# Operand sums of the second FFN weight, made between the steps of the projections instead of inside the FFN loop

## The chip, the cores and the metric

One core of one Trainium2 chip runs the kernel. The metric is the device time in microseconds (us); of several runs, the median. Engines: TensorE (PE; its weight loads PEld), VectorE (DVE), ScalarE (ACT), GpSimd (POOL), and SyncE (SP), which here only issues transfers.

## What is computed

One layer of an encoder with 1024 tokens and 16 meta tokens ahead of them, width 1024, in float32: neighbourhood attention (8 heads) beside gated linear attention (GLA, 4 heads), then an FFN with a convolution of width 3 over the tokens and a gate.

```python
u = rmsnorm(h, norm_mix_pre)
proj = u @ w_in
o_na = rmsnorm(neighbourhood_attention(q_na, k_na, v_na, rpb), na_gain)
o_gl = gla_bidirectional(q_gl, k_gl, v_gl, g_gl, z_gl, ...)   # per direction, chunks of 64:
#   ds = einsum(k_end, v); S[n+1] = decay[n] * S[n] + ds[n]; o = a @ v + q_dec @ S
h = h + rmsnorm(concat(o_na, o_gl) @ w_o, norm_mix_post)
a = conv3(rmsnorm(h, norm_ffn_pre) @ w_ffn_in)                # 2 * 2816 columns
y = (gelu(a[:, 2816:]) * a[:, :2816]) @ w_ffn_out
return (h + rmsnorm(y, norm_ffn_post))[16:]
```

## The kernel before, in words

Large products are float32 split in a high and a low part, three products each. A program of named steps writes the work; a scheduler with a time model then sets each engine's order, and each engine runs its own list in order.

**Projections and heads** (0 to some 374 us). `load_w` (L157) brings blocks of w_in by SP in two halves, `split` makes high and low parts (ScalarE L148, VectorE L149). The tuple `T0` (L67) gives the order of the steps: "gqk" projects queries and keys of a pair of GLA heads (products pk, pq; ScalarE copies them to gst at L347, VectorE multiplies at L350), "exp" makes decays (GpSimd L322 to L327 write bl and ga), "head" is `gla_head` (L357): GpSimd zeroes two columns of the state tile S (L365, L366), TensorE transposes keys (gtm, gt) and makes the 16 chunk products (gd), VectorE runs the scan over the chunks in both directions (L396 on partitions 0 to 63, L400 on 64 to 127, 15 operations each on 64x128), and TensorE takes the states for gom (L409) and go (L429, L432). go begins with a matmul of zeros (zbf, L425). "qk" and "v" are projections of the neighbourhood heads; `v_windows` (L489) copies values to vw_d in HBM by SP.

**FFN loop** (`for j`, L1113; some 690 to 1098 us). The first FFN weight is multiplied by a seven-product scheme over 22 column blocks j. `prep` makes operand sums bt (GpSimd L941 to L944) and splits them (ScalarE L922, VectorE L924). TensorE makes the products (L966 to L968) into q_r, q_x, q_z; ScalarE evicts (c, L1079), VectorE adds (L1130, L1140, L1146), convolves (L1014, L1015) and multiplies by the gelu (ScalarE L1025) at L1026; y goes to y_d.

**Operand sums of the second weight.** The second product, too, is made by seven products per pair of blocks, from y_d, s_d (sums of y) and t_d (sums of w_ffn_out). After each odd j, `t_sums(j // 2)` (L1085) loads two blocks of 512 KB of w_ffn_out by SP (L1088), makes four differences in place on GpSimd (L1090 to L1093, 128x512 each) and stores both to t_d by SP (L1095); `s_sums` (L1097) does the like with y. The tiles come from a ring of six, tag "y", which also holds y. There are eleven calls. t_d is read only in the sweeps after the loop, from 1098 us on.

Of the kernel before, what the change touches and what calls it, by code (L numbers as in the profile page):

```python
# [8 lines left out]
F32 = mybir.dt.float32  # L9
F32R = mybir.dt.float32r  # L10
BF16 = mybir.dt.bfloat16
# [4 lines left out]
P = 128  # L16
# [7 lines left out]
NFC = FF // P  # L24
# [26 lines left out]
def _mask_offsets():  # L51
# [13 lines left out]

PRIO = {(0, 0): 5, (0, 2): 20, (0, 3): 2, (1, 0): 1, (1, 2): 60, (1, 3): 2, (2, 1): 20, (2, 3): 5, (3, 2): 1, (3, 3): 60}
T0 = (  # L67
    "gqk 0", "head 0", "qk 2", "exp 2", "head 1", "exp 3", "qk 0", "v 0", "gqk 1", "head 2", "qk 1", "head 3",
    "n15",
)  # L70
T1 = ("qk 3", "na 0 0", "na 0 1", "v 1", "na 1 0", "na 1 1")
T2 = (
# [10 lines left out]
def kernel(ctx: ExitStack, tc: tile.TileContext, a: dict):  # L83
    nc = tc.nc
    mm = nc.tensor.matmul
# [7 lines left out]
    t_d = [dram.tile([2, 2, P, 512], F32, name=f"t_d{k}") for k in range(NFC // 2)]  # L93
# [60 lines left out]
    ul = up.tile([P, KC, L], F32R, name="ul")  # L154
    wp = t1.enter_context(tc.tile_pool(name="wp", bufs=3))

    def load_w(src, w, name):  # L157
        hs, ls = [], []
        for kh in range(2):
            raw = wp.tile([P, 4, 256], F32, tag="wr", name=f"{name}_r{kh}", bufs=2)  # L160
            nc.sync.dma_start(raw[:, :, :w], src[:, 4 * kh : 4 * kh + 4, :])
            hi = wp.tile([P, 4, 256], F32R, tag="wh", name=f"{name}_h{kh}")
            lo = wp.tile([P, 4, 256], F32R, tag="wl", name=f"{name}_l{kh}")
            split(hi[:, :, :w], lo[:, :, :w], raw[:, :, :w])
            hs.append(hi)
            ls.append(lo)
        return hs, ls
# [40 lines left out]
    with tc.tile_pool(name="p1", bufs=2) as p1:  # L208
        g_pre = p1.tile([P, D], F32, name="g_pre", bufs=1)
        nc.sync.dma_start(g_pre, a["norm_mix_pre"].broadcast_to([P, D]))  # L210
        for i in range(9):
            n = NM if i == 0 else P
# [46 lines left out]
    gwh = gp.tile([P, HGL, P], F32R, name="gwh")  # L259
    gwl = gp.tile([P, HGL, P], F32R, name="gwl")  # L260
    split(gwh, gwl, gwr)
    zbf = gp.tile([P, 512], BF16, name="zbf")
    nc.gpsimd.memset(zbf, 0.0)
    maskf = gp.tile([P, 512], I8, name="maskf")
    maskv = maskf.rearrange("p (t c) -> p t c", c=P)
# [5 lines left out]
    d0 = gp.tile([P, L], BF16, name="d0")  # L271
# [85 lines left out]
    def gla_head(hd):  # L357
# [53 lines left out]
        for g in range(2):  # L411
            at = asb[g]
            pf = ps_s(f"gaf{hd}_{g}")
            pb = ps_s(f"gab{hd}_{g}")
            for t in range(4):
                c = slice(NM + (4 * g + t) * P, NM + (4 * g + t + 1) * P)
                mm(pf[:, t * P : (t + 1) * P], B[:64, c], C[:64, c], start=True, stop=True)
                mm(pb[:, t * P : (t + 1) * P], B[64:, c], C[64:, c], start=True, stop=True)
            atv = at.rearrange("p (t c) -> p t c", c=P)
            pbv = pb.rearrange("p (t c) -> p t c", c=P)  # L420
            nc.scalar.copy(atv[:64, :, :64], pbv[:64, :, :64])
            nc.scalar.copy(atv[64:, :, 64:], pbv[64:, :, 64:])
            nc.vector.copy_predicated(at, maskf, pf)
            po = ps_c(f"go{hd}_{g}")
            mm(po, zbf[:, :P], zbf, start=True, stop=False, skip_group_check=True)  # L425
            for t in range(4):
                i = 4 * g + t
                tc_ = slice(t * P, (t + 1) * P)
                mm(po[:, tc_], V[:, i, :], at[:, tc_], start=False, stop=False, skip_group_check=True)  # L429
                for s in range(2):  # L430
                    cc = NM + i * P + 64 * s
                    mm(  # L432
                        po[:, t * P + 64 * s : t * P + 64 * s + 64],
                        S[:, 2 * i + s + 1, :],
                        C[:, cc : cc + 64],
                        start=False,
                        stop=(t == 3 and s == 1),
                        skip_group_check=True,
                    )
            gla_norm(po, mgl[:, hd, 1 + 512 * g : 513 + 512 * g], 512, f"gn{hd}_{g}")  # L440
# [48 lines left out]
    def v_windows(half):  # L489
        vv = v_d[:, 256 * half : 256 * half + 256].rearrange("(r c) d -> r c d", c=64)  # L490
        for b in range(4):
            nr, r0 = BNR[b], BR0[b]
            for q in range(4):
# [5 lines left out]
                else:  # L499
                    nc.sync.dma_start(dst[0], vv[0, cols, :])  # L500
                    nc.sync.dma_start(dst[1:], vv[r0 + 1 : r0 + 1 + nr, cols, :])

    hs, ls = load_w(a["w_in_b"][5], 256, "wvg1")
    pv = lambda i0, i1: [proj_v1(i, hs, ls, vg_d, 256, "pvg1") for i in range(i0, i1)]
    gla_gate(0)
# [13 lines left out]
    def step1(name):  # L519
        op, *n = name.split()  # L520
        n = [int(x) for x in n]
        if op == "na":
            na_step(*n)
        elif op == "n15":
            gla_norm(o15s, mgl[:, :, 0], HGL, "gn15")
        elif op == "v":
            na_v(n[0], na_meta if n[0] else None)
        else:
            steps[op](*n)

    for name in T0:
        step1(name)
    t1r.close()

    frp = ctx.enter_context(tc.tile_pool(name="frp", reuse_waits="tile", bufs=1, side="right"))

# [545 lines left out]
    def ring4(name):  # L1082
        return fc.tile([P, 4, 256], F32, tag="y", name=name, bufs=6)

    def t_sums(k):  # L1085
        w = [ring4(f"w{k}_{c}").rearrange("p (h d) b -> p h (d b)", h=2) for c in range(2)]
        for c in range(2):
            nc.sync.dma_start(w[c], a["w_ffn_out"][2 * k + c].rearrange("h p d -> p h d"))  # L1088
        b11, b12, b21, b22 = w[0][:, 0], w[0][:, 1], w[1][:, 0], w[1][:, 1]
        nc.gpsimd.tensor_sub(b11, b12, b11)  # L1090
        nc.gpsimd.tensor_sub(b12, b22, b12)
        nc.gpsimd.tensor_sub(b22, b22, b11)
        nc.gpsimd.tensor_sub(b21, b21, b22)  # L1093
        for c in range(2):
            nc.sync.dma_start(t_d[k][c].rearrange("h p d -> p h d"), w[c])  # L1095

    def s_sums(k, p, q):  # L1097
        (a11, a21), (a12, a22) = p, q
        nc.gpsimd.tensor_add(a22, a21, a22)
# [13 lines left out]
    for j in range(1, NFC):  # L1113
        if j == NFC - 1:
            t = mixp.tile([P, 8, HC], F32, tag="m", name="pre1")
            raws = [t[:, x, :512] for x in range(8)]
            for w in (4, 5):
                t = quad(w, f"pre{w}", F32)
                raws += [t[:, x, :512] for x in range(4)]
            for k in range(8):  # L1120
                pre.append(raws[2 * k : 2 * k + 2])
                nc.sync.dma_start(pre[k][0], y_d[2 * k][0])
                nc.sync.dma_start(pre[k][1], a["w_ffn_out"][2 * k][0])
        R, X = acc1[j, "r"], acc1[j, "x"]
        c11 = evac("c11", j, "r")
        y = ring4(f"y{j}")
        y = [y[:, :2], y[:, 2:]]
        ys.append(y)
        prod(j, 6, "r", False)
        nc.vector.tensor_add(c11, X[:, :, :258], c11)  # L1130
        c12 = evac("c12", j, "r")
        prod(j, 5, "z", True)
        Z = acc1[j, "z"]
        conv(j, 0, c11, y[0])
        prod(j, 7, "r", False)
        c22 = evac("c22", j, "r")
        if j < NFC - 1:
            prep(j + 1)
            prod(j + 1, 1, "r", True)
        nc.vector.tensor_add(c22, Z[:, :, :258], c22)  # L1140
        prod(j, 4, "r", False)
        if j < NFC - 1:
            prod(j + 1, 2, "x", True)
        prod(j, 3, "z", False)
        conv(j, 0, R[:, :, :258], y[1])
        nc.vector.tensor_add(c12, Z[:, :, :258], c12)  # L1146
        gated(j, 1, c22, y[1])
        gated(j, 0, c12, y[0])
        store(y_d[j], y)
        if j % 2:  # L1150
            t_sums(j // 2)
            s_sums(j // 2, ys[j - 1], y)
    fcs.close()
    fas.close()
# [260 lines left out]
```

## Time and profile before

| | us |
|---|---|
| median of 3 runs (lowest, highest) | 1353.88 (1353.38, 1354.87) |
| the profiled execution | 1352.37 |
| its span, first to last instruction | 1350.7 |

| engine | busy, us | share of the span |
|---|---|---|
| PE | 1268.2 | 94% |
| DVE | 914.0 | 68% |
| ACT | 619.3 | 46% |
| POOL | 429.7 | 32% |

The mean granted TensorE clock is 0.973 of full speed. Shares are averages over stages with different limits, so they are read stage by stage: a timeline gives each instruction's start and length and, in brackets, how long its engine sat idle before it and what released it. "SPq" and the like are an engine's sequencer issuing transfers.

### The profile page before, as it was taken

What the parts mean: (1) busy time and instruction counts of PE and PEld (TensorE: products, weight loads), DVE (VectorE), ACT (ScalarE), POOL (GpSimd) and SP (SyncE); (2) the same over time, 40 slices, a digit from 0 to 9 for tenths busy, and PEclk for the clock granted to TensorE, in tenths of its full rate; (3) what the DMA queues carried; (4) which work ended last, traced back from release to release, by engine and by line L of the source; (5) the groups of instructions that cost most, each with busy time, mean ns of one, the idle gap of its engine ahead of it and who ended that gap; (6) DMA issues with size and microseconds to landing.
All of it is one profiled execution on the core that took longest, in us unless ns stands there. A gap on an engine that the chain in (4) does not pass through costs nothing.

```text
span 1350.7 us, 23581 instructions
## 1 busy us (share of the span) xinstructions
PE 1268.2 (94%) x9048; PEld 1139.0 (84%) x9050; DVE 914.0 (68%) x1453; ACT 619.3 (46%) x1198; POOL 429.7 (32%) x401
## 2 busy tenths in 40 slices
PE   7979999999997899998779999999999999999997
PEld 6869888988886587776779999999999998888876
DVE  6491365254544577865979898898888978555556
ACT  5443544152332555656544444344443444545542
POOL 1260001000021154432556565765657633000001
PEclk9989999999988889999889999999999999999999
DMA  6311132351187545842134434444344456866735
GB/s 204 119 38 50 34 93 84 110 177 64 51 270 225 208 132 197 278 137 94 40 117 149 142 124 164 167 154 143 124 164 159 154 173 228 303 198 207 247 125 187
DMA packets 117137, 203.74 MB, mean 151 GB/s; under 512 B 18080, under 2 KB 51200, under 8 KB 117024
## 3 DMA queue, kind: packets, MB, share of 16 engines
q1 hardware_dynamic: 117024, 202.24, 44.6%
q8 instruction: 71, 1.16, 0.4%
q14 instruction: 42, 0.34, 0.1%
HBM read 145.64 MB, written 66.19 MB: 157 GB/s over the span
## 4 chain that ended last, share of the span: by engine, by line
PE 63%; DVE 18%; DMA 6%; ACT 5%; issue 5%; POOL 1%; SPq 1%; DVEq 0%; ACTq 0%; POOLq 0%
DVE bl L924 5%; PE bank L1202 4%; PE bank L1201 4%; PE bank L1200 4%; PE q_r L966 3%; PE q_r L967 3%; PE q_r L968 3%; PE ops L694 2%; PE pna L175 2%; PE pna L176 2%; PE pna L177 2%; DVE g L1015 2%; PE pp L688 2%; PE wo L766 2%; PE wo L767 2%
## 5 line engine op out<-in xcount | busy, mean ns | idle before, releaser
L966 PE MATMUL q_r<-ah,bh 128*128 128x258 f32 x504 | 145.4, 288 | 14.9 <-ACT c L1079 14.9
L967 PE MATMUL q_r<-al,bh 128*128 128x258 f32 x504 | 144.3, 286 | 0.0
L968 PE MATMUL q_r<-ah,bl 128*128 128x258 f32 x504 | 143.9, 285 | 0.0
L966 PEld LDWEIGHTS q_r<-ah,bh 128*128 128x128 f32 x504 | 97.1, 193 | 17.2 <-ACT c L1079 17.1
L149 DVE TENSOR_TENSOR ol<-r,oh 128x512 fp32r<-128x512 f32 x116 | 74.6, 688 | 46.0 <-ACT oh L148 46.0
L1200 PE MATMUL bank<-oh,oh 128*128 128x512 f32 x264 | 102.9, 390 | 2.2 <-DVE c L1266 2.2
L1201 PE MATMUL bank<-oh,ol 128*128 128x512 f32 x264 | 102.7, 389 | 0.0
L1202 PE MATMUL bank<-ol,oh 128*128 128x512 f32 x264 | 102.2, 389 | 0.0
L966 PE MATMUL q_z<-ah,bh 128*128 128x258 f32 x336 | 95.4, 284 | 6.3 <-DVE y L1015 4.9
L1025 ACT ACTIVATE g<-g 128x512 f32<-128x512 f32 (+1 forms) x46 | 28.2, 614 | 157.0 <-DVE g L1015 156.9
L967 PEld LDWEIGHTS q_r<-al,bh 128*128 128x128 f32 x504 | 97.0, 193 | 0.0
L968 PEld LDWEIGHTS q_r<-ah,bl 128*128 128x128 f32 x504 | 97.0, 192 | 0.0
L967 PE MATMUL q_z<-al,bh 128*128 128x258 f32 x336 | 95.2, 283 | 0.0
L968 PE MATMUL q_z<-ah,bl 128*128 128x258 f32 x336 | 95.0, 283 | 0.0
L148 ACT CAST oh<-r 128x512 fp32r<-128x512 f32 x116 | 65.6, 619 | 50.2 <-PE bank L1201 40.0
L924 DVE TENSOR_TENSOR bl<-bt,bh 128x512 fp32r<-128x512 f32 x84 | 85.2, 1015 | 3.5 <-ACT bh L922 3.5
L924 DVE TENSOR_TENSOR bl<-fr,bh 128x512 fp32r<-128x512 f32 x67 | 64.5, 966 | 17.4 <-ACT bh L922 17.2
L1011 ACT ACTIVATE g<-c,vec 128x512 f32<-128x512 f32 (+1 forms) x46 | 36.6, 795 | 75.2 <-DVE c L1140 40.8
L966 PEld LDWEIGHTS q_z<-ah,bh 128*128 128x128 f32 x336 | 63.9, 190 | 6.7 <-issue 5.1
L144 POOL TENSOR_TENSOR rsc_r<-rsc_v,nhalf 128x1 f32<-128x1 f32 x8 | 5.8, 725 | 197.5 <-DVE rsc_v L143 197.5
L1014 DVE SCALAR_TENSOR_TENSOR g<-c,vec,g 128x512 f32<-128x512 f32 (+1 forms) x46 | 53.5, 1164 | 17.1 <-ACT g L1011 17.1
L1026 DVE TENSOR_TENSOR y<-y,g 128x512 f32<-128x512 f32 (+1 forms) x46 | 54.9, 1194 | 13.4 <-ACT g L1025 13.3
(388 smaller groups left out, 4257.9 us busy)
## 6 DMA issues: line engine op xcount, KB each, us to landing
fr<-in_w_ffn_in_dram SPq DMA_DIRECT2D x44, 512.0 KB
y_d<-y SPq DMA_DIRECT2D x44, 256.0 KB
w<-in_w_ffn_out_dram SPq DMA_DIRECT2D x22, 512.0 KB
t_d<-w SPq DMA_DIRECT2D x22, 512.0 KB
s_d<-y SPq DMA_DIRECT2D x44, 256.0 KB
r<-s_d SPq DMA_DIRECT2D x44, 256.0 KB
r<-t_d SPq DMA_DIRECT2D x44, 256.0 KB
r<-y_d SPq DMA_DIRECT2D x25, 256.0 KB
```

The lines of the kernel that those rows point to most:

```text
L148: nc.scalar.copy(hi, src)
L149: nc.vector.tensor_tensor(lo, src, hi.bitcast(F32), ALU.subtract)
L924: nc.vector.tensor_tensor(lo, src, hi.bitcast(F32), ALU.subtract)
L966: mm(ps, w[0][:, k, :], A[0][:, k, c], start=(first and k == 0), stop=False, skip_group_check=True)
L967: mm(ps, w[0][:, k, :], A[1][:, k, c], start=False, stop=False, skip_group_check=True)
L968: mm(ps, w[1][:, k, :], A[0][:, k, c], start=False, stop=(last and k == 3), skip_group_check=True)
L1011: nc.scalar.activation(dst, tap(1), AF.Identity, bias=col(VEC_CB + ch), scale=col(VEC_CONV + 2 * NFC + ch))
L1014: nc.vector.scalar_tensor_tensor(dst, tap(0), col(VEC_CONV + ch), dst, ALU.mult, ALU.add)
L1026: nc.vector.tensor_mul(val, val, g)
L1200: mm(ps, A[0][:, tk], B[0], start=first, stop=False, skip_group_check=True)
L1201: mm(ps, A[1][:, tk], B[0], start=False, stop=False, skip_group_check=True)
L1202: mm(ps, A[0][:, tk], B[1], start=False, stop=last, skip_group_check=True)
```

## The change

`t_sums` moves out of the loop. In `T0` there are twelve new steps "t 0" to "t 11" between the old ones. Step "t k" first stores set k - 1 from ScalarE's queue (L517), then loads set k on SP behind the last weight load (L523) and makes the four differences on GpSimd (L525 to L528). `issue_after` ties a transfer to the place of the named instruction in the program, so that the scheduler does not move it ahead. The tiles are a pool of their own, four of 128x2x512, that is two sets of two; it is closed after the stage. To make room, zbf shrinks to 128 columns, and the zeroing matmul takes d0 as its other operand.

```diff
 T0 = (
-    "gqk 0", "head 0", "qk 2", "exp 2", "head 1", "exp 3", "qk 0", "v 0", "gqk 1", "head 2", "qk 1", "head 3",
-    "n15",
+    "gqk 0", "t 0", "head 0", "t 1", "qk 2", "t 2", "exp 2", "head 1", "t 3", "exp 3", "t 4", "qk 0", "t 5", "v 0",
+    "t 6", "t 7", "gqk 1", "t 8", "head 2", "t 9", "qk 1", "t 10", "head 3", "t 11", "n15",
 )
...
-            nc.sync.dma_start(raw[:, :, :w], src[:, 4 * kh : 4 * kh + 4, :])
+            w_last[0] = nc.sync.dma_start(raw[:, :, :w], src[:, 4 * kh : 4 * kh + 4, :]).ins
...
-    zbf = gp.tile([P, 512], BF16, name="zbf")
+    zbf = gp.tile([P, P], BF16, name="zbf")
...
-            mm(po, zbf[:, :P], zbf, start=True, stop=False, skip_group_check=True)
+            mm(po, zbf, d0[:, :512], start=True, stop=False, skip_group_check=True)
...
+    tws = ExitStack()
+    twp = tws.enter_context(tc.tile_pool(name="twp", reuse_waits="tile", bufs=1))
+    twt = {}
+
+    def last(engine):
+        traced = nc.cur_bb.bb.instructions
+        return next(i for i in reversed(traced) if i.engine == engine)
+
+    def t_sums(k):
+        if k:
+            with tc.issue_after(last(mybir.EngineType.Activation)):
+                for c in range(2):
+                    nc.scalar.dma_start(t_d[k - 1][c].rearrange("h p d -> p h d"), twt[k - 1, c])
+        if k == NFC // 2:
+            return
+        with tc.issue_after(w_last[0]):
+            for c in range(2):
+                twt[k, c] = twp.tile([P, 2, 512], F32, tag="tw", name=f"tw{k}_{c}", bufs=4)
+                nc.sync.dma_start(twt[k, c], a["w_ffn_out"][2 * k + c].rearrange("h p d -> p h d"))
+        b11, b12, b21, b22 = twt[k, 0][:, 0], twt[k, 0][:, 1], twt[k, 1][:, 0], twt[k, 1][:, 1]
+        nc.gpsimd.tensor_sub(b11, b12, b11)
+        nc.gpsimd.tensor_sub(b12, b22, b12)
+        nc.gpsimd.tensor_sub(b22, b22, b11)
+        nc.gpsimd.tensor_sub(b21, b21, b22)
...
-    def t_sums(k):
-        w = [ring4(f"w{k}_{c}").rearrange("p (h d) b -> p h (d b)", h=2) for c in range(2)]
...
-        for c in range(2):
-            nc.sync.dma_start(t_d[k][c].rearrange("h p d -> p h d"), w[c])
...
         if j % 2:
-            t_sums(j // 2)
             s_sums(j // 2, ys[j - 1], y)
```

Where it moves instructions, by the two programs' orders (after the change the lines of the stage stand two further on, those of the FFN 18 to 30). GpSimd around head 1, before: ga2 and ga3 are the last decays, gs1 and gs2 the states of heads 1 and 2.

```order
L326 TENSOR_TENSOR ga2_2070<-bl2_2072,gc2_910 128x16
L327 TENSOR_TENSOR ga2_2070<-bl2_2072,gc2_910 128x1024
L365 MEMSET gs1_2088 64x128
L366 MEMSET gs1_2088 64x128
L326 TENSOR_TENSOR ga3_2249<-bl3_2251,gc3_989 128x16
L327 TENSOR_TENSOR ga3_2249<-bl3_2251,gc3_989 128x1024
L365 MEMSET gs2_2951 64x128
L366 MEMSET gs2_2951 64x128
```

The same place after the change (tw2_0 is the first tile of set 2):

```order
L328 TENSOR_TENSOR ga2_2101<-bl2_2103,gc2_913 128x16
L329 TENSOR_TENSOR ga2_2101<-bl2_2103,gc2_913 128x1024
L367 MEMSET gs1_2119 64x128
L368 MEMSET gs1_2119 64x128
L525 TENSOR_TENSOR tw2_0_2093<-tw2_0_2093 128x512
L328 TENSOR_TENSOR ga3_2290<-bl3_2292,gc3_992 128x16
L329 TENSOR_TENSOR ga3_2290<-bl3_2292,gc3_992 128x1024
L526 TENSOR_TENSOR tw2_0_2093<-tw2_1_2095,tw2_0_2093 128x512
L527 TENSOR_TENSOR tw2_1_2095<-tw2_1_2095,tw2_0_2093 128x512
L528 TENSOR_TENSOR tw2_1_2095<-tw2_1_2095 128x512
L525 TENSOR_TENSOR tw3_0_2282<-tw3_0_2282 128x512
L526 TENSOR_TENSOR tw3_0_2282<-tw3_1_2284,tw3_0_2282 128x512
```

One sum of set 2 stands ahead of ga3, and eleven of sets 2 to 4 (five are shown) between it and head 2's memset.

GpSimd ahead of head 2's end, after the change; before, nothing stood between the memsets of gs2 and gs3:

```order
L525 TENSOR_TENSOR tw8_0_3030<-tw8_0_3030 128x512
L528 TENSOR_TENSOR tw7_1_2806<-tw7_1_2806 128x512
L526 TENSOR_TENSOR tw8_0_3030<-tw8_1_3032,tw8_0_3030 128x512
L527 TENSOR_TENSOR tw8_1_3032<-tw8_1_3032,tw8_0_3030 128x512
L528 TENSOR_TENSOR tw8_1_3032<-tw8_1_3032 128x512
L525 TENSOR_TENSOR tw9_0_3205<-tw9_0_3205 128x512
L526 TENSOR_TENSOR tw9_0_3205<-tw9_1_3207,tw9_0_3205 128x512
L527 TENSOR_TENSOR tw9_1_3207<-tw9_1_3207,tw9_0_3205 128x512
L528 TENSOR_TENSOR tw9_1_3207<-tw9_1_3207 128x512
```

The first sum of set 8 stands ahead of the last one of set 7.

ScalarE around the second pair's keys, before (pvn: values, gst: the keys' copy):

```order
L148 CAST wqk1_h1_2739<-wqk1_r1_2737 128x1024
L148 CAST wna1_h0_3114<-wna1_r0_3112 128x1024
L195 COPY pvn0_s8_2704<-pvn0_8_2679 128x256
L347 ACTIVATE gst2_0_False_2768<-pk1_0_2743 64x272 x2
L347 ACTIVATE gst3_0_False_2773<-pk1_0_2743 64x272 x2
```

and after:

```order
L148 CAST wqk1_h1_2820<-wqk1_r1_2818 128x1024
L148 CAST wna1_h0_3215<-wna1_r0_3213 128x1024
L197 COPY pvn0_s8_2765<-pvn0_8_2740 128x256
L517 DMA t_d5_110<-tw5_0_2496 128x2x512
L517 DMA t_d5_110<-tw5_1_2498 128x2x512
L517 DMA t_d6_111<-tw6_0_2794 128x2x512
L517 DMA t_d6_111<-tw6_1_2796 128x2x512
L349 ACTIVATE gst2_0_False_2849<-pk1_0_2824 64x272 x2
```

Four stores, two sets, stand between the last value copy and the first gst.

GpSimd in the FFN loop, before, sums of y (y2, y3), of the second weight (w2) and of the first (bt7):

```order
L1101 TENSOR_TENSOR y2_7751<-y3_7992,y2_7751 128x512
L1102 TENSOR_TENSOR y3_7992<-y3_7992,y2_7751 128x512
L1090 TENSOR_TENSOR w2_0_8731<-w2_0_8731 128x512
L1091 TENSOR_TENSOR w2_0_8731<-w2_1_8732,w2_0_8731 128x512
L1092 TENSOR_TENSOR w2_1_8732<-w2_1_8732,w2_0_8731 128x512
L941 TENSOR_TENSOR bt7_5_8841<-fr7_1_8835,fr7_0_8833 128x512
L1093 TENSOR_TENSOR w2_1_8732<-w2_1_8732 128x512
L942 TENSOR_TENSOR bt7_6_8842<-fr7_1_8835,bt7_5_8841 128x512
L943 TENSOR_TENSOR bt7_7_8843<-fr7_1_8835 128x512
```

and after:

```order
L1119 TENSOR_TENSOR y2_7855<-y3_8096,y2_7855 128x512
L1120 TENSOR_TENSOR y3_8096<-y3_8096,y2_7855 128x512
L971 TENSOR_TENSOR bt7_5_8925<-fr7_1_8919,fr7_0_8917 128x512
L972 TENSOR_TENSOR bt7_6_8926<-fr7_1_8919,bt7_5_8925 128x512
L973 TENSOR_TENSOR bt7_7_8927<-fr7_1_8919 128x512
L974 TENSOR_TENSOR bt7_4_8928<-fr7_0_8917,bt7_6_8926 128x512
```

The four operations on w are gone from between those on y and bt. VectorE's order is unchanged; TensorE's differs in the operand of eight matmuls alone.

## Rows read from the trace of the kernel before

**Rows 1.** Stretches, core 0: us, busy us (x instructions), granted clock, DMA share, GB/s

```profile
200.00:374.00 174.00, 173.65 (x1260) 156.08 (x1261) 82.18 (x178) 61.46 (x117) 5.85 (x11) 1.00 0.31 99
...
720.00:1098.00 378.00, 365.31 (x3012) 363.23 (x3011) 339.00 (x361) 169.12 (x288) 232.22 (x141) 1.00 0.43 150
```

**Rows 2.** Timeline, TensorE, ahead of and in the FFN loop: start, us, engine, line, operation [idle before, releaser]

```profile
686.36 0.55 PE L966 MATMUL q_z<-ah,bh 128*128 128x258 f32 x1 [4.91 <-DVE y L1015]
...
778.25 0.35 PE L966 MATMUL q_r<-a,bh 128*128 128x258 f32 x1 [0.88 <-DVE y L1015]
...
959.04 0.56 PE L966 MATMUL q_r<-ah,bh 128*128 128x258 f32 x1 [1.88 <-ACT c L1079]
...
1086.14 0.39 PE L966 MATMUL q_r<-ah,bh 128*128 128x258 f32 x1 [0.53 <-ACT c L1079]
```

**Rows 3.** Timeline, VectorE, one pair of column blocks

```profile
868.70 1.78 DVE L924 TENSOR_TENSOR bl<-bt,bh 128x512 fp32r<-128x512 f32 x1
...
874.38 0.68 DVE L924 TENSOR_TENSOR bl<-fr,bh 128x512 fp32r<-128x512 f32 x1
874.98 0.68 DVE L1140 TENSOR_TENSOR c<-q_z,c 128x516 f32<-128x516 f32 x1
```

**Rows 4.** Timeline, GpSimd, the same place

```profile
868.18 1.74 POOL L1093 TENSOR_TENSOR w<-w 128x512 f32<-128x512 f32 x1
```

**Rows 5.** Stretches behind the pauses of 4.91 and 1.88 us

```profile
686.30:696.30 10.00, 7.05 (x31) 6.78 (x32) 7.69 (x9) 3.98 (x7) 4.61 (x3) 0.50 0.38 132
...
959.00:962.50 3.50, 3.46 (x16) 3.46 (x17) 2.62 (x6) 1.81 (x3) 1.59 (x1) 0.51 0.92 311
```

**Rows 6.** Timeline, SP and GpSimd: a pair of 512 KB loads and its first user

```profile
1068.76 0.98 SPq L1088 DMA_DIRECT2D w<-in_w_ffn_out_dram  x2
...
1072.75 1.29 POOL L1090 TENSOR_TENSOR w<-w 128x512 f32<-128x512 f32 x1 [4.38 <-DMA w<-in_w_ffn_out_dram]
```

**Rows 7.** Timeline, ScalarE: rows ahead of the stores of sets 0, 1, 7

```profile
200.12 0.63 ACT L449 ACTIVATE gn_r<-gn_r 128x512 f32<-128x512 f32 x1
...
208.05 0.58 ACT L148 CAST qst<-pna 128x512 fp32r<-128x512 f32 x1
...
295.28 2.42 ACT L347 ACTIVATE gst_True<-pq 64x512 f32<-64x512 f32 x4
```

**Rows 8.** Timeline, VectorE and GpSimd: a scan alone, and beside GpSimd

```profile
79.17 2.32 DVE L313 TENSOR_TENSOR_SCAN gc<-d,gt_b 64x1040 f32<-64x1040 bf16 x1
...
90.42 4.02 DVE L313 TENSOR_TENSOR_SCAN gc<-d,gt_b 64x1040 f32<-64x1040 bf16 x1
...
90.36 1.90 POOL L327 TENSOR_TENSOR ga<-bl,gc 128x1024 f32<-128x1024 f32 x1
```

**Rows 9.** Timeline, VectorE: state scans of heads 1 and 2

```profile
214.11 0.33 DVE L396 SCALAR_TENSOR_TENSOR gs<-gs,dec 64x128 f32<-64x128 f32 x1
...
225.83 1.51 DVE L400 SCALAR_TENSOR_TENSOR gs<-gs,dec 64x128 f32<-64x128 f32 x4
...
311.52 1.13 DVE L400 SCALAR_TENSOR_TENSOR gs<-gs,dec 64x128 f32<-64x128 f32 x3
```

**Rows 10.** Timeline, TensorE: where it takes the scans' results

```profile
227.49 0.35 PE L409 MATMUL gom<-gc,gs 128*128 128x1 f32 x2
...
313.85 0.22 PE L432 MATMUL go<-gc,gs 128*128 128x64 f32 x1
```

**Rows 11.** Timeline, SP: window copies of the values

```profile
282.45 8.18 SPq L501 DMA_DIRECT2D vw_d<-v_d  x8
```

**Rows 12.** Timeline, GpSimd and VectorE near 673 us

```profile
673.57 7.90 POOL L944 TENSOR_TENSOR bt<-fr,bt 128x512 f32<-128x512 f32 x1 [13.65 <-DVE bl L924]
...
676.22 1.23 DVE L1057 TENSOR_TENSOR s<-u2b,u2a 128x1024 f32<-128x1024 f32 x1
```

**Rows 13.** Timeline, ScalarE and SP ahead of the second pair's keys

```profile
273.03 1.62 ACT L347 ACTIVATE gst_False<-pk 64x272 f32<-64x272 f32 x4 [1.82 <-PE pk L177]
...
270.55 1.54 SPq L498 DMA_DIRECT2D vw_d<-v_d  x2
```

More of the change, by code (lines that the diff above doesn't have):

```diff
@@ L155 @@
     wp = t1.enter_context(tc.tile_pool(name="wp", bufs=3))
+    w_last = [None]
     def load_w(src, w, name):
@@ L525, in step1 @@
             gla_norm(o15s, mgl[:, :, 0], HGL, "gn15")
+        elif op == "t":
+            t_sums(*n)
         elif op == "v":
@@ L533 @@
     t1r.close()
+    tws.close()
     frp = ctx.enter_context(tc.tile_pool(name="frp", reuse_waits="tile", bufs=1, side="right"))
@@ L1083, in ring4 @@
         return fc.tile([P, 4, 256], F32, tag="y", name=name, bufs=6)
-    def t_sums(k):
-        w = [ring4(f"w{k}_{c}").rearrange("p (h d) b -> p h (d b)", h=2) for c in range(2)]
-        for c in range(2):
[L1088 to L1094, printed above, removed]
-            nc.sync.dma_start(t_d[k][c].rearrange("h p d -> p h d"), w[c])
     def s_sums(k, p, q):
```

## The prediction

> **What bounds the kernel now.** I read the stretches first [rows 1], then TensorE's timeline through the FFN loop for its pauses [rows 2], then VectorE and GpSimd there side by side [rows 3, 4], and last the projection stage, where the operand sums are to go, with the same two engines in mind.
>
> The stretches show two different stages. From 200 to 374 us (projections and heads) TensorE is busy for 173.65 of 174.00 us, GpSimd for 5.85 [rows 1]. A free GpSimd invites work, but a TensorE without a gap means that anything late there costs time at once. From 720 to 1098 us (FFN loop) TensorE is busy for 365.31 of 378.00 us, VectorE for 339.00, GpSimd for 232.22 [rows 1]. The missing 12.69 us are ten pauses; the first, the longest and the last stand in [rows 2], below one from ahead of the loop. Eight of the ten end with an eviction of ScalarE, 0.53 to 1.88 us each; that eviction stands behind the gelu, which waits for VectorE. So the loop is TensorE-bound with a pause of about 1.4 us in each pair of column blocks that VectorE sets.
>
> Why VectorE is late is in its own rows: the subtraction of L924, two operands in SBUF, takes 0.68 us alone and 1.78 us while GpSimd has a tensor_tensor of its own under way [rows 3, 4]. GpSimd's starting at 868.18 ends at 869.92 [rows 4], and VectorE's from 868.70 ends 0.56 us later. They take turns: each GpSimd operation costs VectorE 1.78 - 0.68 = 1.10 us. An operation that reads PSUM at the same time is not slowed (0.68 us at 874.98) [rows 3].
>
> **The gain: sums out of the loop.** 44 GpSimd operations, 22 loads and 22 stores leave the FFN part. Some nine of the eleven sets lie in this stretch. Four operations at 1.10 us could take up to 9 x 4 x 1.10 = 39.6 us off VectorE's 339.00, which then lies further below TensorE's 365.31 [rows 1]; the sums on s_d and the operand sums of the first weight stay. I expect the eight pauses behind evictions to go, and keep the two that VectorE's y ends (0.88 and 0.91 us; the first is in [rows 2]): 12.69 - 1.8 = 10.9 us. The 1.88 us pause is followed by 3.50 us at a granted clock of 0.51 [rows 5], 1.7 us of work lost, which goes with it. Gain: **12.6 us**. Bounds: 8 (a third of the pauses stays, since y's own sums contend as before) and 12.69 + 1.7 = 14.4. The loads and stores that leave the loop gain nothing: no pause ends at a transfer.
>
> **The cost: where the sums land.** GpSimd is in order, each set waits for its load, the load for a free tile, the tile for a store that now stands in ScalarE's order. All of that is TensorE-paced, so I place it on the old time axis. A pair of 512 KB transfers takes 1072.75 - 1068.76 = 4.0 us [rows 6].
>
> Head 1. Set 0's stores stand behind ScalarE's L449 that ends at 200.75, set 1's behind the cast that ends at 208.63 [rows 7]. Set 2 loads at 204.8 and has its data at 208.8; set 3 loads at 212.6 and has it at 216.6. Set 2's first sum now stands ahead of the ga of the last head, so its three others start at about 212.5 (208.8, one sum of some 1.5, and the ga's 2.1; its large operation takes 1.90 [rows 8]). At 1.5 us an operation (taking turns with VectorE's 0.38), GpSimd is then busy with sets 2 and 3 to about 222.6. Set 4 takes set 3's tiles, whose stores wait for that: 4.0 + 4.0 us later is 230.6, too late to matter. Meanwhile VectorE runs the head's scan over 16 chunk states, from 214.11 to 227.34 [rows 9]: 30 small operations on 64 partitions, two operands in SBUF each. TensorE wants its last state for gom at 227.49 [rows 10], so the slack is 0.15 us. Of the seven, six fall in the scan: 6 x 1.10 - 0.15 = **6.4 us**, bounds 0 and 7 x 1.10 = 7.7.
>
> Head 2. Set 7's stores follow the gst copies that end at 297.70 [rows 7]; set 9's loads start at 301.7, data at 305.7: four operations. Set 8's second load stands on SP behind eight copies that end at 290.63 [rows 11], data at about 295; its last operation ends near 299.8. The scan ends at 312.65 [rows 9], TensorE goes on at 313.85 [rows 10], slack 1.20. Five operations: 5 x 1.10 - 1.20 = **4.3 us**, bounds 0 and 5.4. Sets 0 and 1 are done before head 0's scan; set 10 falls ahead of head 3's, costed at nothing, at most 2 x 1.10.
>
> That such a scan can suffer at all is a choice. For it: L313's scan over 64 partitions takes 2.32 us alone and 4.02 us while GpSimd's 1.90 us ga runs [rows 8]. Against it: at 673.57 a GpSimd tensor_tensor lasted 7.90 us while VectorE ran on at full pace (1.23 us for 1024 columns) [rows 12]. There GpSimd paid. That VectorE run overlaps its starts with the ends before them; the state scan does not (0.34 us at a pitch of 0.38), which is nearer to turns, so I take 1.10. The Trainium skill has a rule on it (SBUF — State Buffer, Who interferes with whom): VectorE's second port pair is GpSimd's, an exclusive lock, held for an operation by whoever has it. By that rule the state scans wait for whole sums and the sum stands; the row at 673.57 shows that the lock need not change hands each time, which would make the cost of both heads nothing.
>
> ScalarE's queue. The 22 stores are 22 issues in its order; two such issues on SP take 0.98 us [rows 6] and ScalarE is busy for 61.46 of 174 us [rows 1], so it hides. But set 6's two stores share completion semaphores with SP's vw_d copies, and stand ahead of the first gst, at 273.03 [rows 13], whose product must leave PSUM before TensorE's transposes. Those copies are issued from 270.55 to 272.09 [rows 13]; at the 4.0 us of [rows 6] they end at 276.1, so ScalarE would stand 3.1 us longer than now. TensorE's share is between 0 and 3.1; I take **1.5 us**.
>
> The clock. The long pauses are followed by a stretch at half speed in this trace: 3.50 us at 0.51 after 1.88 us, 10.00 us at 0.50 after 4.91 us [rows 2, 5]. So each long pause costs 1.7 to 5.0 us more. Where VectorE trickles on and TensorE waits in parts it may be less; I take the smaller price for two heads: **3.4 us**, bounds 0 and 10.
>
> The smaller zero tile costs nothing: eight matmuls of the same shape take another operand, and one memset gets shorter. SP's 22 loads move into the projections, behind the last weight load each; the products of the half before cover the next half's load, so I cost them at nothing (cover gone: one load's 4.0 us [rows 6]).
>
> Sum: 6.4 + 4.3 + 1.5 + 3.4 = 15.6 lost, 12.6 gained: **+3.0 us** on the profiled execution, 1352.37 us (span 1350.7 and 1.67 around it): 1355.4. That execution lies 1.5 us below the median of the runs, 1353.88; against the median it is **1356.9 us**. A difference under 0.2%, 2.7 us, can't be told from none.
>
> **Rivals.** *VectorE keeps the port* (not slower). Place: the scans of heads 1 and 2, as at 673.57 [rows 12]. With the eleven sums at a price p the loss is 11p - 1.35 + 1.5 + 3.4, which is less than 12.6 below p = 0.82 us: from there on the change gains. At p near nothing both heads and their clock cost nothing and the 1.5 us remain: 1353.88 - 12.6 + 1.5 = 1342.8 us. At half the price, heads 3.2 + 1.6 and clock 1.7 make 1353.88 - 12.6 + 8.0 = 1349.3.
>
> *The loop keeps its pauses.* VectorE stays late through y's sums and L941 to L944, which take the same turns; against it speaks how little it is late, 1.4 us a pair. With 4 of the 12.6 us gained: 1353.88 + 15.6 - 4 = 1365.5 us.
>
> *ScalarE's queue decides.* A store that waits for its sum or semaphore holds up gst and the head's copies behind it; with the port free but 3.1 us and a long half-clock stretch of 5.0 behind it: 1353.88 - 12.6 + 8.1 = 1349.4 us.
>
> **Chances.** The forecast 0.50, with its own range of 1349 to 1364 from the bounds of its terms (faster 0.10, same 0.17, slower 0.23). VectorE keeps the port, wholly or by half, 0.32 (faster 0.29, same 0.03). The loop keeps its pauses 0.12 (slower 0.12). The queue 0.06 (faster 0.04, same 0.02). Sum: faster 0.43, same 0.22, slower 0.35. The range takes in the second case and most of the third: 1340 to 1365.
>
> **What would show it.** Right: the pauses in the loop behind the c eviction gone and GpSimd's busy time there down by some 55 us; a pause of TensorE ahead of gom in heads 1 and 2, with L398/L402 operations of 1.4 us beside GpSimd's L525 to L528, and a granted clock near 0.5 behind it. Wrong: a scan at 0.38 pitch with GpSimd operations stretched to several us (the first rival); pauses of the loop as before (the second); TensorE waiting for ScalarE's gst near 275 us (the third).

## The result, and the profile after

The change makes the kernel slower: 1368.27 us, the median of 14 runs (1356.74 to 1373.11), against 1354.06 us for the kernel before in its 14 (1351.71 to 1356.34); the ratio is 1.0094 (1.0078 to 1.011). The prediction's sum had the direction, while its chances leaned the other way (faster 0.43, slower 0.35). The size was not forecast: +14.2 us between the medians against +3.0, and 1368.3 us lies outside the range. The profiled execution took 1366.51 us, 14.1 more than that of before.

The stretches first, of the kernel after, columns as in [rows 1] (us, busy us of PE, PEld, DVE, ACT, POOL, then the granted clock, DMA share, GB/s). 735 to 1113 us is the FFN stretch that lay at 720 to 1098 before.

```profile
200.00:374.00 174.00, 159.58 (x1050) 142.25 (x1049) 78.57 (x134) 52.86 (x98) 55.14 (x45) 0.89 0.59 201
735.00:1113.00 378.00, 378.00 (x3155) 378.00 (x3154) 324.38 (x378) 181.26 (x302) 173.90 (x108) 1.00 0.30 105
```

In the loop TensorE is now busy for 378.00 of 378.00 us, and GpSimd's 232.22 has become 173.90: every pause is gone, the two behind VectorE's y as well. In the projections 173.65 us of TensorE have become 159.58, and the clock 1.00 has become 0.89.

If each matmul of before is set beside the same one of after, the lag grows from 0.6 us near 200 to 32.3 us at 352, stays within 31.2 to 32.7 to the loop, and falls to 13.4 by 1131. So some **32 us were lost in the heads and 19 gained in the loop**. By place, the lag grows by 11.2 us at head 1's scan, 3.7 at the value copies, 7.1 at gtm, 1.2 at gaf and 8.7 at head 2's scan. The pauses are in TensorE's timeline of after:

```profile
228.00 0.39 PE L177 MATMUL pna<-uh,wna_h 128*128 128x272 f32 x1 [1.77 <-DVE qst L464]
...
232.20 0.69 PE L434 MATMUL go<-gc,gs 128*128 128x64 f32 x2 [2.07 <-DVE gs L402]
...
269.48 0.39 PE L190 MATMUL pvn<-wvn_h,uh 128*128 128x256 f32 x1 [1.91 <-ACT pvn_s L197]
...
295.71 0.38 PE L372 MATMUL gtm<-ident,ga 128*16 128x128 f32 x1 [4.43 <-DVE ga L352]
...
311.95 0.48 PE L419 MATMUL gaf<-gc,gb 64*128 64x128 f32 x2 [1.16 <-DVE gc L352]
...
339.55 0.39 PE L177 MATMUL pna<-uh,wna_h 128*128 128x272 f32 x1 [2.26 <-DVE qst L464]
```

A seventh, 0.77 us at 341.08, ends with the scan as the one at 232.20 does. The pauses at 228.00, 232.20, 339.55 and 341.08 (6.9 us together) belong to the scans of heads 1 and 2: L464 is a small operation that stands in VectorE's order among the scan's last, L402 the scan itself. Those at 269.48 and 295.71 (6.3 us) belong to queues. The one at 311.95 (1.16 us) belongs to the sums again, at a place that was not foreseen: sums of sets 7 and 8 run beside VectorE's products of L352 for the second pair, three of which take 1.77 us (0.69 in the kernel before), and gaf waits for the one behind them.

```profile
309.77 1.77 DVE L352 TENSOR_TENSOR gb<-gb,gst_False 128x512 f32<-128x512 f32 x1
309.26 1.74 POOL L528 TENSOR_TENSOR tw<-tw 128x512 f32<-128x512 f32 x1
```

The four stretches behind pauses, of the kernel after:

```profile
232.30:247.00 14.70, 14.70 (x63) 13.47 (x64) 0.83 (x3) 3.00 (x6) 5.55 (x6) 0.51 0.22 72
269.50:274.00 4.50, 4.50 (x25) 4.50 (x26) 0.42 (x1) 0.00 (x0) 2.91 (x4) 0.62 0.64 205
295.70:303.00 7.30, 7.29 (x23) 5.88 (x24) 2.55 (x7) 2.00 (x6) 0.00 (x0) 0.62 1.01 390
341.00:353.00 12.00, 11.88 (x53) 10.81 (x54) 0.54 (x3) 0.73 (x2) 0.00 (x0) 0.57 0.09 32
```

At a clock of 0.51 a stretch of 14.70 us loses 0.49 of itself. The four lose 7.2 + 1.7 + 2.8 + 5.2 = **16.9 us**, more than the 14.4 us of all seven pauses.

VectorE in head 1's scan, kernel after:

```profile
219.94 0.35 DVE L402 SCALAR_TENSOR_TENSOR gs<-gs,dec 64x128 f32<-64x128 f32 x1
220.32 1.27 DVE L398 SCALAR_TENSOR_TENSOR gs<-gs,dec 64x128 f32<-64x128 f32 x1
221.62 1.34 DVE L402 SCALAR_TENSOR_TENSOR gs<-gs,dec 64x128 f32<-64x128 f32 x1
223.00 1.34 DVE L398 SCALAR_TENSOR_TENSOR gs<-gs,dec 64x128 f32<-64x128 f32 x1
224.38 1.35 DVE L402 SCALAR_TENSOR_TENSOR gs<-gs,dec 64x128 f32<-64x128 f32 x1
225.76 0.34 DVE L398 SCALAR_TENSOR_TENSOR gs<-gs,dec 64x128 f32<-64x128 f32 x1
```

and GpSimd beside it:

```profile
220.07 1.37 POOL L525 TENSOR_TENSOR tw<-tw 128x512 f32<-128x512 f32 x1 [3.65 <-DMA tw<-in_w_ffn_out_dram]
...
224.28 1.30 POOL L528 TENSOR_TENSOR tw<-tw 128x512 f32<-128x512 f32 x1
```

They take turns, one for one: four sums, four scan operations of 1.27 to 1.35 us in place of 0.35, 1.0 us each. Four sums, not six, met the full scan of head 1 (set 3's; set 2's came as it began), and four that of head 2.

The queues. ScalarE of the kernel after (ACTq is its sequencer, issuing stores):

```profile
269.05 0.37 ACT L197 COPY pvn_s<-pvn 128x256 f32<-128x256 f32 x1 [9.58 <-DMA v_d<-pvn_s]
...
286.48 7.79 ACTq L517 DMA_DIRECT2D t_d<-tw  x3
294.31 3.20 ACT L349 ACTIVATE gst_False<-pk 64x272 f32<-64x272 f32 x8 [7.63 <-DMA vw_d<-v_d]
```

and SP's own queue ahead of the first of these:

```profile
259.50 0.34 SPq L199 DMA_DIRECT2D v_d<-pvn_s  x1
265.54 0.38 SPq L523 DMA_DIRECT2D tw<-in_w_ffn_out_dram  x1
266.01 0.42 SPq L202 DMA_DIRECT2D v_d<-pvn_s  x1
```

gst starts 7.63 us after ScalarE's last copy, some 5.8 us after its first product was done (the matmul at 288.18 ends at 288.47). Three stores stand ahead of it in ScalarE's order, and what ends the wait is SP's window copies. And the value store at 266.01 stands on SP behind a load at 265.54 that waited for its tile, that is for a store out of ScalarE's order (three such waits of SP between 240 and 310 us, 9.7 us in all); the value copy at 269.05 waited for that value store.

### The profile page after: what moved, and what is told of

It reads as the page before. It is cut to its first block, busy times and chain, and to the rows that moved or that the text cites. A ratio compares the mean times of both kernels' runs of the same rounds, so it can differ in the third digit from the quotient of the medians.

```text
span 1364.8 us, 23575 instructions
## 1 busy us (share of the span) xinstructions
PE 1278.9 (94%) x9050; PEld 1148.3 (84%) x9050; DVE 894.8 (66%) x1453; ACT 623.2 (46%) x1198; POOL 414.3 (30%) x401
## 3 DMA queue, kind: packets, MB, share of 16 engines
q8 instruction: 71, 1.16, 0.3%
## 4 chain that ended last, share of the span: by engine, by line
PE 75%; DVE 10%; DMA 8%; ACT 3%; issue 2%; SPq 1%; POOL 1%; DVEq 0%; ACTq 0%; POOLq 0%
PE q_r L996 6%; PE q_r L997 6%; PE q_r L998 6%; PE bank L1219 4%; PE bank L1217 4%; PE bank L1218 4%; PE q_z L996 3%; PE q_z L997 3%; PE q_z L998 3%; DMA v_d<-pvn_s 2%; PE ops L724 2%; PE pna L177 2%; PE pna L178 2%; PE pna L179 2%; PE pp L718 2%; PE wo L796 2%
## 5 line engine op out<-in xcount | busy, mean ns | idle before, releaser
L971 POOL TENSOR_TENSOR bt<-fr,fr 128x512 f32<-128x512 f32 x21 | 32.3, 1537 | 165.1 <-DMA fr<-in_w_ffn_in_dram 122.6
L954 DVE TENSOR_TENSOR bl<-bt,bh 128x512 fp32r<-128x512 f32 x84 | 74.8, 892 | 3.6 <-ACT bh L952 3.6
L177 PE MATMUL pna<-uh,wna_h 128*128 128x272 f32 (+2 forms) x192 | 63.5, 331 | 4.0 <-DVE qst L464 4.0
L178 PE MATMUL pna<-ul,wna_h 128*128 128x272 f32 (+2 forms) x192 | 64.3, 335 | 0.0
```

Of the source, the lines that this page charges most:

```text
L177: mm(ps[:m, :n], wh, uh[:, k, t0 : t0 + n], start=(k == 0), stop=False)
L178: mm(ps[:m, :n], wh, ul[:, k, t0 : t0 + n], start=False, stop=False)
L954: nc.vector.tensor_tensor(lo, src, hi.bitcast(F32), ALU.subtract)
L971: nc.gpsimd.tensor_sub(f[5], b12, b11)
```

## The experiments

Each ran against the kernel before on the same chip; the median of before beside them was 1353.77 to 1355.04 us, and the ratios are to it.

**Neither sums nor their transfers.** From the kernel before:

```diff
-            t_sums(j // 2)
-        6: lambda k: (s_d[2 * k][0], t_d[k][1][1]),
+        6: lambda k: (s_d[2 * k][0], a["w_ffn_out"][2 * k + 1][1]),
```

and so for the other three operands out of t_d.

> The kernel before without the operand sums of the second weight, nowhere made; the sweeps read w_ffn_out itself in their place (same sizes), so the result of the second product is another. Theory: the loop's share of the change is what the trace after shows, about 19 us from 720 us to the end of the loop, so about 1335 us, with no pause behind the c eviction. Rival: it is the 12.6 us of the forecast and the rest of the trace's 19 came from work that only moved; then about 1341 us.

Measured: 1335.52 us, ratio 0.9861 (0.9843 to 0.9879). The theory held: the loop's part of the change is worth 18.2 us, half as much again as forecast.

**Transfers without sums.** From the kernel after, the four `nc.gpsimd.tensor_sub` of `t_sums` left out.

> The kernel after with its loads and stores of the operand sums, but without the 44 subtractions (t_d gets plain weights). Theory of two causes: the pauses ahead of go in heads 1 and 2 (5.1 and 3.4 us) and their half-clock stretches (6.8 and 5.1 us) go, the pauses behind ScalarE's value copy and gst and their half clock (about 12 us) stay: about 1348 us. Rival, GpSimd's turns are all of the loss: about 1336 us. Rival, the queues are all of it: about 1368 us as before.

Measured: 1344.44 us (0.9912 to 0.9948 of before). Both causes are there: 1368.3 - 1344.4 = 23.9 us go with the sums, 1344.4 - 1335.5 = 8.9 us remain with the transfers. TensorE's timeline of this run keeps two pauses between 200 and 380 us, and none at go:

```profile
258.47 0.57 PE L190 MATMUL pvn<-wvn_h,uh 128*128 128x256 f32 x1 [2.47 <-ACT pvn_s L197]
...
284.25 0.38 PE L372 MATMUL gtm<-ident,ga 128*16 128x128 f32 x1 [3.97 <-DVE ga L352]
```

**Loads and sums without stores.** From the kernel after, with w_ffn_out read in place of t_d:

```diff
         if k:
-            with tc.issue_after(last(mybir.EngineType.Activation)):
-                for c in range(2):
-                    nc.scalar.dma_start(t_d[k - 1][c].rearrange("h p d -> p h d"), twt[k - 1, c])
+            pass
```

> The kernel after with loads and subtractions, but no store of the sums; the sweeps read w_ffn_out itself instead. A load now waits for subtractions alone, and ScalarE issues nothing. Theory of two causes: the pauses at the value copy and gst and their half clock go (about 12 us); the sums come earlier, so that the scans of heads 1 and 2 meet between none and four of them: 1340 to 1356 us. Rival, stores matter nothing: about 1368 us.

Measured: 1351.72 us over 10 runs from 1347.44 to 1356.34. Within the span given, but it tells little: the loads came earlier, and the sums met other scans. TensorE still paused at go and gom, and at gaf for a product of VectorE (3.6 us in two pauses). The pause at gst went, as expected; the one at the value copies did not (1.5 us, with no store at all), so the stores are not its only cause.

**The sums left in the loop, after the even blocks.** From the kernel before:

```diff
         if j % 2:
-            t_sums(j // 2)
             s_sums(j // 2, ys[j - 1], y)
+        if j > 1 and (j % 2 == 0 or j == NFC - 1):
+            t_sums((j - 1) // 2)
```

> The kernel before with the operand sums left in the FFN loop, but made after the even column blocks, and the sums of y after the odd ones as now: four sums of each kind in each half of a pair in place of eight in one. Nothing is left out. Theory: the pause of each pair comes from eight sums in one half; spread, VectorE stays below TensorE in both and the pauses go: 1335 to 1342 us. Rival: VectorE's work over the whole pair sets the pause, then about 1354 us as before.

Measured: 1356.49 us (1.0001 to 1.0033). The theory fell, and the waits of TensorE between 720 and 1098 us in this run say how: the pauses moved, from the c eviction to VectorE's y, and their sum stayed (12.69 us before).

```profile
PE q_r L966 <- DVE y L1015: 12.8, 10, 1.8
```

(us in total, times, longest.) The even half holds fewer than four more sums.

**Sums left in the loop, two and two.** From the kernel before; `t_first` loads a set and makes its first two sums, `t_second` the other two and the stores; `last_pool()` is GpSimd's last instruction so far.

```diff
         if j % 2:
-            t_sums(j // 2)
+            if j == 1:
+                t_first(0)
+            with tc.issue_after(last_pool()):
+                t_second()
             s_sums(j // 2, ys[j - 1], y)
+        else:
+            with tc.issue_after(last_pool()):
+                t_first(j // 2)
```

> The kernel before with the operand sums left in the FFN loop, two of a set's four after an even column block and two after the next odd one, ahead of the sums of y; nothing is left out. Theory: each half of a pair has a slack of its own. The odd half is over it by 1.57 us with eight sums behind it, so two fewer (2 x 1.10) clear it; the even half is over it by 1.4 us with four (the run with all four there), so two clear it as well: all pauses go, 1336 to 1342 us. Rival: VectorE's sum over the pair decides, then 1353 to 1357 us as with the four moved together.

Measured: 1344.36 us, ratio 0.9932 (0.9909 to 0.9954), faster than both kernels with the whole computation done. The same waits in this run:

```profile
PE q_r L966 <- DVE y L1015: 3.4, 7, 1.2
```

So it is neither the pair's total nor one half's: each half takes about two sums, and 12.7 us of pauses fall to 3.4. The time is 2 us above the span given; two pauses of before at the end of the loop remain, one of them longer (2.19 us in place of 1.40).

**Two sets in the projections.** The kernel after with "t 0" to "t 2" only (the last stores set 1); the other nine sets in the loop as before.

> The kernel after with only sets 0 and 1 made in the projections (both done before head 0's scan), the other nine in the loop as before. Theory: these two cost nothing there, and two pairs lose their pause of 1.9 us each: about 1350 us. Rival: transfers in the projections cost by themselves, whatever the place: 1354 us or more.

Measured: 1350.62 us, ratio 0.9976 (0.9959 to 0.9993). The time is as expected, and in the profile the heads have no pause: sets that meet no scan cost nothing there. That each takes a pause out of the loop is not shown. The two pauses at VectorE's y are gone, but eight behind the c eviction remain, and the total is hardly less (12.69 us before); the first is 0.61 us in place of 1.57, two late ones are 1.58 and 1.54 in place of 0.60 and 0.53. The profiled execution took 1352.47 us, no less than that of before, so the trace does not show where the other runs gained. Its waits between 720 and 1098 us:

```profile
PE q_r L996 <- ACT c L1109: 11.8, 8, 1.8
```

**Transfers without sums, stores on SP.** From the second run:

```diff
-            with tc.issue_after(last(mybir.EngineType.Activation)):
+            with tc.issue_after(w_last[0]):
                 for c in range(2):
-                    nc.scalar.dma_start(t_d[k - 1][c].rearrange("h p d -> p h d"), twt[k - 1, c])
+                    nc.sync.dma_start(t_d[k - 1][c].rearrange("h p d -> p h d"), twt[k - 1, c])
```

> The kernel after without the 44 subtractions (as in the run before it of that kind, 1344.4 us), and with the stores on SP's queue, each behind the last weight load, in place of ScalarE's. Theory: the pause of 3.97 us ahead of gtm and its half clock come from ScalarE standing at stores ahead of gst; with the stores on SP it goes, the one behind the value copy (SP's own order) stays: 1338 to 1340 us. Rival: the late window copies themselves hold up the keys, or SP blocks more than ScalarE did: 1344 us or more.

Measured: 1335.66 us, the same as with no transfers at all (1335.52). The pause at gtm is gone. Of the value copy's, 1.90 us remain in its profile: TensorE is 2.8 us behind the kernel before from there to 380 us and 0.9 us at 760, so it is made up ahead of the loop and leaves nothing in the time; the expectation of 1338 to 1340 was too high. The same bytes move in both runs, and all 8.8 us went with the stores' place in ScalarE's order. The small zero tile, which this kernel has and the first of these runs has not, costs nothing either. ScalarE in this run:

```profile
275.87 1.62 ACT L349 ACTIVATE gst_False<-pk 64x272 f32<-64x272 f32 x4 [0.63 <-PE pk L179]
```

**Head 1 left free.** The kernel after; sets 2 and 3 are loaded and stored, not summed:

```diff
+        if k in (2, 3):
+            return
         nc.gpsimd.tensor_sub(b11, b12, b11)
```

> The kernel after, but sets 2 and 3, whose sums meet head 1's scan, are loaded and stored without being summed. Theory: the pauses of head 1 (about 5 us) and the half-clock stretch behind them (6.8 us) go, those of head 2 and of the queues stay: about 1356 us. Rival: the half clock comes anyhow, at the next pause; then only some 5 us go, about 1363 us.

Measured: 1358.98 us over 10 runs (1354.4 to 1363.43), 9.3 us below the kernel after; the pauses and the clock of head 1 went together (the pause at gtm is longer in this run, 6.30 us in place of 4.43). The stretches of this run that answer to the slow one behind 232.30:

```profile
225.00:232.00 7.00, 6.96 (x54) 6.52 (x54) 2.95 (x10) 1.30 (x3) 2.68 (x3) 1.00 0.65 209
232.00:247.00 15.00, 15.00 (x97) 12.59 (x96) 5.38 (x7) 5.90 (x9) 2.97 (x5) 1.00 0.51 167
```

**All sums, stores on SP.** The kernel after, its sums kept, with the edit of "Transfers without sums, stores on SP".

> The kernel after with all its sums, the stores on SP's queue, each behind the last weight load, in place of ScalarE's; nothing is left out. Theory: the causes add up. The runs without sums lost 8.8 us by ScalarE's stores, so 1368.3 - 8.8 = 1359.5 us, with the pauses of the heads as after. Rival: SP, which now also waits for the sums, holds up value stores and weights: 1365 us or more.

Measured: 1357.04 us (1351.92 to 1366.93), ratio 1.0023 (0.9998 to 1.0048). The sum of causes fits, but not for the reason given: with the stores elsewhere the loads came at other times, and the sums met L352's products near 164 us and the scans of heads 0 (four sums from 179.8 us) and 1, while head 2's went free. Against the run with the same stores and no sums, 1335.7 us, the sums cost 21.4 us. TensorE's waits in this run, 200 to 395 us:

```profile
PE pna L177 <- DVE qst L464: 4.2, 1, 4.2
PE pvn L190 <- ACT pvn_s L197: 1.7, 1, 1.7
PE go L434 <- DVE gs L402: 1.0, 1, 1.0
```

**Combined.** Stores on SP; sets 0 and 1 ahead of head 0, sets 2 and 3 behind head 1, seven sets split in the loop. `gate` is SP's last transfer so far.

```diff
+    "gqk 0", "t 0", "head 0", "t 1", "qk 2", "exp 2", "head 1", "exp 3", "qk 0", "t 2", "t 3", "v 0", "t 4",
+    "gqk 1", "head 2", "qk 1", "head 3", "n15",
...
+        gate = last(mybir.EngineType.SP) if k > 1 else w_last[0]
...
+        elif j // 2 >= NT0:
+            with tc.issue_after(last_pool()):
+                t_first(j // 2)
```

> Nothing is left out. Sets 0 and 1 in the projections ahead of head 0's scan, sets 2 and 3 between the scans of heads 1 and 2 (their loads behind SP's last query store of the step ahead), all stores on SP; sets 4 to 10 in the loop, two sums after an even block and two after the next odd one, as in the split run. Theory: away from the scans a sum costs nothing, and the split costs (1344.4 - 1335.5) / 11 = 0.8 us a set, so 1335.5 + 7 x 0.8 = 1341 us (1339 to 1343). Rival: in the projections even sums outside the scans cost, through the turns with the key products of the second pair or through SP's order: 1346 us or more.

Measured: 1345.45 us, ratio 0.9942 (0.9922 to 0.9963): no better than the split alone. In its profile no scan is touched; the value copies lose 1.4 us of pauses, and the end of the loop is late.

**The same, the loop's sets two pairs earlier** (`t_first(j // 2 + 2)`).

> The combined kernel with the loop's seven sets begun two pairs earlier (after even blocks 4 to 16 in place of 8 to 20); nothing is left out. Theory: of the 10 us that the combined run lies above the run without sums, about 4 come at the loop's end, where the last set meets the last sums of y (a pause of 3.11 us behind the c sum); with the last pairs free they go: 1340 to 1342 us. Rival: that pause is the last sums of y themselves, and the time stays at 1344 to 1346 us.

Measured: 1345.81 us, ratio 0.9932 (0.9914 to 0.9949). The time is the rival's, its mechanism is not: with the last pairs free the pause is gone from the profile, so it was the sums' (kernels whose last pair makes these sums pause there for 1.40 to 3.11 us, those whose last pair makes none do not). What it gave back is lost elsewhere. On the axis of the kernel before, this profile is 3.3 us behind the combined one at 1090 us, 1.5 us ahead at 1120 and 1.0 us behind at the end; in the sweeps behind the loop TensorE waits longer for VectorE's c. The waits behind 1098 us, combined and then this run:

```profile
PE bank L1247 <- DVE c L1313: 0.4, 1, 0.4
...
PE bank L1247 <- DVE c L1313: 2.7, 2, 1.8
```

Why it loses more ahead of 1090 us and in the sweeps was not tried.

**Two sets in the projections, nine split** (stores on SP, `t_first(j // 2 + 1)`).

> Nothing is left out. Only sets 0 and 1 in the projections (stores on SP); sets 2 to 10 in the loop, split in two and two, begun one pair early (after even blocks 2 to 18), so that the last pair has none. Theory: the value copies are not held up (about 1 us less than with sets 2 and 3 there), nine split sets cost 0.4 to 0.8 us each: 1339 to 1343 us. Rival: the splits' pauses add up over nine pairs: 1345 us or more.

Measured: 1342.9 us, ratio 0.9909 (0.9893 to 0.9925): the lowest median of the versions that do all the work, 11 us below the kernel before and 25 below the change; as expected. Its interval overlaps that of the split alone. Its TensorE waits in the loop, and in the heads from 200 to 374 us, are

```profile
PE q_r L998 <- DVE y L1047: 4.2, 8, 1.3
...
PE go L432 <- issue: 0.3, 2, 0.2
```

## Why the prediction was right or wrong

*The turns.* Right. "They take turns" was read from the FFN loop [rows 3, 4] and carried over to a scan that had never met a sum; 1.10 us a sum was forecast, 1.0 was measured, and the row at 673.57 [rows 12], the basis of the first rival, did not repeat in the scans. (Two rows were read as "alone" that are not quite: at 79.17 GpSimd copies single columns beside the scan, at 874.38 its next sum starts 0.22 us later.) The rule of the Trainium skill on the shared port pair (SBUF — State Buffer, Who interferes with whom), an exclusive lock for a whole instruction, agrees with the rows of head 1: the scan operation of 224.38 ends at 225.73, 0.15 us behind the sum of 224.28. Fewer sums met the scans, four where six and five were counted; others met L352, which was not thought of. The pauses are 6.9 us in the heads and 1.2 at gaf, 8.0 in all, against 10.7.

*The clock.* **The step that failed most.** "I take the smaller price for two heads: 3.4 us" stood for what four stretches show as 16.9 us, 12.4 of them in the two heads and 4.5 behind pauses at queues. The price was taken from one short stretch behind a pause of 1.88 us, although the row beside it, 10.00 us at 0.50 [rows 5], was as near (a second pause, of 2.89 us, lies in it, which the prediction did not see); and no clock was counted behind the queues. Head 1's run shows that its pauses and its slow clock are one term: without its sums both went, 9.3 us for 3.8 us of pauses.

*ScalarE's queue.* Right in place, too small: 1.5 us were taken (bounds 0 and 3.1), and pauses of 6.3 us with slow stretches came. Two things were missed. The window copies themselves came later than in the profile of before, so that ScalarE stood for 7.63 us: SP issued the last of them 2.1 us behind gst's first product (290.58 and 288.47 us), before the change 0.9 us ahead of it. And SP stood, too: "I cost them at nothing" was said of its loads, but a load that waits for a tile holds the value stores behind it. The two runs without sums price the stores' order on ScalarE: 8.8 us. What holds the value copies is open in part, since their pause stays with the stores on SP (1.9 us) and without any (1.5 us). The Trainium skill has issuing from another engine save a little issue time and no more (DMA: Bandwidth & Descriptors, Issuing engines are not separate DMA queues); of what it can cost the engine that issues, these two runs are the measure here.

*The gain.* Right in kind, low: 12.6 us forecast (bounds 8 and 14.4), 18.2 measured. Eight pauses were added up by the idle time that the rows print. A pause costs more, as the kernel before shows around one of them:

```profile
788.06 0.29 PE L968 MATMUL q_x<-ah,bl 128*128 128x258 f32 x1
788.18 0.28 PE L966 MATMUL q_x<-ah,bh 128*128 128x258 f32 x1
790.04 0.39 PE L966 MATMUL q_r<-ah,bh 128*128 128x258 f32 x1 [1.57 <-ACT c L1079]
790.27 0.28 PE L967 MATMUL q_r<-al,bh 128*128 128x258 f32 x1
```

From start to start it is 1.86 us and then 0.23, against 0.12 for each within a run: 1.85 us lost where the bracket says 1.57. And the two pauses behind y, kept in the forecast, went as well, 1.8 us, and so did one behind the stretch that the prediction looked at:

```profile
1117.17 0.39 PE L966 MATMUL q_z<-ah,bh 128*128 128x258 f32 x1 [1.40 <-DVE c L1146]
```

With some 0.28 us more for each of eleven pauses, an estimate from the one above, that makes 12.6 + 1.8 + 1.4 + 3.1 = 18.9 us, against the 18.2 measured.

*The rivals.* VectorE did not keep the port, and the loop did not keep its pauses. The third, the queue, came beside the forecast case, not in its place.

*The account.* Forecast +3.0; clock 16.9 - 3.4 = 13.5 more; queue pauses 6.3 - 1.5 = 4.8 more; pauses by sums 10.7 - 8.0 = 2.7 less; gain 18.2 - 12.6 = 5.6 more: 3.0 + 13.5 + 4.8 - 2.7 - 5.6 = 13.0 us, of 14.1 between the two profiled executions. The forecast's own range, 1349 to 1364, was also narrower than its bounds: the terms' upper bounds, 7.7 + 5.4 + 3.1 + 10 us, against the lowest gain of 8 make 1353.88 + 18.2 = 1372.1 us. That would have taken the result in, but by luck: the clock and the queue both went beyond their bounds.

## What to carry to other kernels

Where TensorE runs without a gap, a small lateness can cost its pause and a slow clock behind it, which here was the larger part: price the two together, with the longest such stretch in the trace as the upper bound, since not every pause brought one. An engine with nothing to do is only free if the engine that it takes turns with has no chain that TensorE waits for; look for the chain's slack (0.15 and 1.20 us here), not for the idle engine's. A store put in the order of an engine that evicts PSUM can hold it for what the store waits for, here up to 7.63 us and until copies had landed whose data it does not touch; and before work is moved across stages, spreading it over its own (two sums and two) is worth a run: it gave 10 us here with no new pool.

## What was not expected of the hardware

After pauses of 1.77 and 2.07 us TensorE ran 14.70 us at 0.51 while it was busy throughout, with 63 matmul records of go and the norm; after 4.43 us, its stretch was shorter (7.30 us at 0.62). The length of the pause alone did not set the length of the slow stretch, nor whether there was one: at the value copies a pause of 1.91 us was followed by 4.50 us at 0.62 in the kernel after, and one of 1.90 us by a clock of 1.00 in the run without sums and with the stores on SP; in the loop of before five pauses of 1.57 to 1.59 us left it at 1.00. The runs do not settle what decides.

Kernels with such pauses seem to spread more from run to run: 16.4 us between the lowest and the highest of 14 runs of the kernel after and 15.0 in 10 with its stores on SP, against 4.6 in 14 runs of before (9.2 in another 21). The two kernels without sums spread by 4.1 and 2.1 us, but in four runs each. Which pauses fall long in which run was not looked at.
